# Turning heads and probabilities by VectorE and DRAM instead of by TensorE in a hybrid decoder layer

## The chip, the cores and the metric

The kernel runs on one core of a Trainium2 chip. The metric is device microseconds of one execution. Before the change the median of three runs is 1015.78 us (1015.49 to 1015.84). Engines are named as in the profile: PE is TensorE, DVE is VectorE, ACT is ScalarE, POOL is GpSimd, and SP is SyncE, which only issues transfers here.

## The reference: what is computed

One decoder layer over 256 tokens of width 2048, all in float32. A first RMS norm feeds one product with `w_in` (2048 to 4096 columns). Its columns are queries, keys and values of eight heads of 128, and 1024 columns for a pooling mixer.

```python
h = rms_norm(x, attn_norm_g)
q, k, v, p = jnp.split(h @ w_in, [1024, 2048, 3072], axis=-1)
q = rms_norm(heads(q), q_norm_g)          # per head, over its 128 columns
k = rms_norm(heads(k), k_norm_g)
a = moba_attention(q, k, heads(v), rel_bias)   # one block of 256: causal softmax with a T5 bias
m = multiscale_pool(p, pool_w, pool_scale)     # causal means over 2, 4, 8, 16 tokens, minus p, then a product
x = x + jnp.concatenate([a, m], axis=-1) @ w_out
x = x + conv_ffn(rms_norm(x, ffn_norm_g), w_up, conv_w, conv_b, w_down)
```

With 256 tokens there is one attention block, so every head is plain causal attention: scores `q k^T / sqrt(128)` plus a bias that depends on the distance, softmax, sum over values. The feed-forward part (width 5632, a causal convolution of three taps, a SiLU gate) is not touched by the change.

## The kernel before

**Weights.** All weights lie in DRAM in the order of their use, as 1 MB chunks of 128 x 2048. A chunk goes through four raw buffers (`raws`, transfers issued by SP). For accuracy each is split in two parts of a reduced float32 type: ACT writes the high part `wh` (L121), DVE writes the rest `wl` (L122). There are three buffers of each part. `split(c)` also issues the load of chunk c + 4 into the raw buffer that has come free (`release`).

**Steps.** The program is a list of steps, each with half a chunk of weight products (24 steps for chunks 0 to 11, and so on). At every even step u the split of chunk u/2 + 2 is issued, then what was `deferred` in the step before, then the products of the step, then the hooks that `after(u, f)` put behind it. So the order of each engine is written out by hand through these numbers. An engine executes its instructions in this order, and a waiting instruction holds all behind it on its engine.

**First part of the layer.** Steps 0 to 15 multiply x with 1024 columns at once, for all of the values v. Steps 16 to 47 are four blocks of eight steps (`tok_block`), each with 512 columns, that is four heads: keys, queries of heads 0 to 3, then keys, queries of heads 4 to 7. Steps 48 to 63 are four groups of pool columns, then come `w_out` and the feed-forward part.

**Attention.** At the end of a block `head_norm` takes the product from PSUM: ACT squares it, DVE sums, a short chain of ACT and DVE makes 1/sqrt, and DVE multiplies into an SBUF tile with tokens on the partitions. The scores need the head's columns on the partitions. `head_T` turns the four heads of a block on PE, eight transposes of 128 x 128 (L371), and ACT copies them out of PSUM with the gain of the norm as its scale (L372). For each head then follow, two steps apart from head to head: `scores` (two products on PE, L383; bias and maximum on DVE, L388; the exponentials on ACT are deferred), `normalise` (DVE, L400 and L402), `probs_T` (three transposes on PE, L409; a copy by ACT, L411) and `head_out` (two products with v, L419 and L420, then a split into the tile `cat` by ACT and DVE). The bias tile T for four heads is loaded by POOL from a small table in DRAM (L293); these eight transfers and the one that writes the table are all that POOL issues.

**Windows.** For each pool group DVE adds up windows of 2 to 16 tokens by doubling (`window_sums`), then `window_mean` multiplies with a table of 1/count (L458) and subtracts the token itself (L459).

## Time and profile before

| | |
|---|---|
| median of three runs | 1015.78 us (1015.49 to 1015.84) |
| profiled execution, its own time | 1015.66 us |
| span of that execution | 1013.9 us |
| granted TensorE clock, mean | 0.999 of full speed |
| PE busy, instructions | 1008.8 us, 5786 |
| DVE busy, instructions | 701.2 us, 760 |
| ACT busy, instructions | 512.5 us, 533 |
| POOL busy, instructions | 13.5 us, 31 |
| moved by transfers | 199.21 MB, mean 196 GB/s |

The span is the time from the first to the last instruction that the profiler saw; the execution's own time holds some start and end around it. Busy time of an engine is the time in which it had at least one instruction in work. The profile also follows the chain that ended last, backwards from the last instruction: at each step to what released it, or to the instruction before it on its engine.

### The profile page before, as it was taken

What the parts mean: (1) busy time and instruction counts of PE and PEld (TensorE: products, weight loads), DVE (VectorE), ACT (ScalarE), POOL (GpSimd) and SP (SyncE); (2) the same over time, 40 slices, a digit from 0 to 9 for tenths busy, and PEclk for the clock granted to TensorE, in tenths of its full rate; (3) what the DMA queues carried; (4) which work ended last, traced back from release to release, by engine and by line L of the source; (5) the groups of instructions that cost most, each with busy time, mean ns of one, the idle gap of its engine ahead of it and who ended that gap; (6) DMA issues with size and microseconds to landing.
All of it is one profiled execution on the core that took longest, in us unless ns stands there. A gap on an engine that the chain in (4) does not pass through costs nothing.

```text
span 1013.9 us, 13827 instructions
## 1 busy us (share of the span) xinstructions
PE 1008.8 (100%) x5786; PEld 887.0 (87%) x5786; DVE 701.2 (69%) x760; ACT 512.5 (51%) x533; POOL 13.5 (1%) x31
## 2 busy tenths in 40 slices
PE   9999999999999999999999999999999999999998
PEld 7888888898888888888888888888888888888888
DVE  6755668967768777777555677777755567777763
ACT  6644455556546555455434455555444445456431
POOL 0300000000000000000000000000000000000000
PEclk9999999999999999999999999999999999999999
DMA  8874454465554655555655555655555555555651
GB/s 338 305 253 166 166 187 167 166 249 208 172 211 175 220 178 206 197 180 193 207 187 202 190 185 189 207 186 197 197 194 202 184 190 194 195 193 180 216 185 42
DMA packets 31182, 199.21 MB, mean 196 GB/s; under 512 B 3640, under 2 KB 4920, under 8 KB 8208
## 3 DMA queue, kind: packets, MB, share of 16 engines
q1 hardware_dynamic: 30544, 196.89, 54.7%
q0 software_dynamic: 576, 1.44, 0.7%
q8 instruction: 45, 0.74, 0.3%
q14 instruction: 17, 0.14, 0.0%
HBM read 195.83 MB, written 2.49 MB: 196 GB/s over the span
## 4 chain that ended last, share of the span: by engine, by line
PE 98%; DMA 1%; SPq 0%; DVE 0%; ACT 0%; issue 0%
PE ps_feat L185 55%; PE ps_feat L187 28%; PE ps_tok L178 9%; PE ps_val L168 4%; PE ps_feat L194 1%; DMA raw<-in_wts 1%; PE ps_pool L194 1%; PE ps_s L383 1%; PE ps_T L371 0%; PE ps_av L419 0%; PE ps_eT L409 0%; SPq L111 0%; PE ps_av L420 0%; SPq L215 0%; PE ps_row L313 0%; DVE wl L122 0%
## 5 line engine op out<-in xcount | busy, mean ns | idle before, releaser
L122 DVE TENSOR_TENSOR wl<-raw,wh 128x2048 fp32r<-128x2048 f32 (+3 forms) x189 | 415.8, 2201 | 196.2 <-ACT wh L121 195.9
L185 PE MATMUL ps_feat<-x2h,wh 128*128 128x512 f32 x1408 | 479.1, 389 | 0.0
L121 ACT ACTIVATE wh<-raw 128x2048 fp32r<-128x2048 f32 (+3 forms) x189 | 348.0, 1842 | 103.3 <-PE ps_feat L185 59.9
L187 PE MATMUL ps_feat<-x2h,wl 128*128 128x256 f32 x1408 | 388.6, 276 | 0.0
L185 PEld LDWEIGHTS ps_feat<-x2h,wh 128*128 128x128 f32 x1408 | 264.3, 188 | 54.9
L187 PEld LDWEIGHTS ps_feat<-x2h,wl 128*128 128x128 f32 x1408 | 264.3, 188 | 0.0
L185 PE MATMUL ps_feat<-hid,wh 128*128 128x512 f32 x680 | 231.3, 389 | 0.0
L187 PE MATMUL ps_feat<-hid,wl 128*128 128x256 f32 x680 | 187.7, 276 | 0.0
L185 PEld LDWEIGHTS ps_feat<-hid,wh 128*128 128x128 f32 x680 | 127.6, 188 | 26.4
L187 PEld LDWEIGHTS ps_feat<-hid,wl 128*128 128x128 f32 x680 | 127.6, 188 | 0.0
L435 ACT ACTIVATE fs<-ps_feat 128x512 f32<-128x512 f32 x75 | 44.9, 598 | 157.3 <-PE ps_feat L187 157.3
L185 PE MATMUL ps_feat<-cat,wh 128*128 128x512 f32 x256 | 87.6, 390 | 0.0
L436 DVE TENSOR_TENSOR fs<-ps_feat,fs 128x512 f32<-128x512 f32 x75 | 51.7, 689 | 49.7 <-ACT fs L435 47.2
L178 PE MATMUL ps_tok<-wh,xh 128*128 128x512 f32 x256 | 82.0, 395 | 0.0
L187 PE MATMUL ps_feat<-cat,wl 128*128 128x256 f32 x256 | 70.7, 276 | 0.0
L677 ACT ACTIVATE hid<-y 128x512 fp32r<-128x512 f32 x22 | 13.9, 632 | 86.2 <-DVE y L676 86.2
L185 PEld LDWEIGHTS ps_feat<-cat,wh 128*128 128x128 f32 x256 | 48.1, 188 | 10.1
L178 PEld LDWEIGHTS ps_tok<-wh,xh 128*128 128x128 f32 x256 | 48.1, 188 | 9.9
L650 ACT ACTIVATE y<-u,pv 128x256 f32<-128x256 f32 x88 | 47.8, 591 | 5.6 <-DVE u L641 5.6
L178 PE MATMUL ps_tok<-wl,xh 128*128 128x512 f32 x128 | 49.9, 390 | 0.0
L187 PEld LDWEIGHTS ps_feat<-cat,wl 128*128 128x128 f32 x256 | 48.0, 188 | 0.0
L664 ACT ACTIVATE y<-y 128x512 f32<-128x512 f32 x22 | 13.9, 632 | 63.9 <-DVE y L653 63.9
(113 smaller groups left out, 681.3 us busy)
## 6 DMA issues: line engine op xcount, KB each, us to landing
raw<-in_wts SPq DMA_DIRECT2D x178, 1024.0 KB, 4.8
raw<-in_wts SPq DMA_DIRECT2D x4, 512.0 KB, 7.5
out<-x SPq DMA_DIRECT2D x7, 256.0 KB, 2.1
xboth<-in_xT SPq DMA_DIRECT2D x6, 256.0 KB, 10.0
T<-band POOLq DMA_DIRECT2D x8, 128.0 KB, 6.2
x<-in_xT SPq DMA_DIRECT2D x1, 1024.0 KB, 9.4
raw<-in_wts SPq DMA_DIRECT2D x3, 256.0 KB, 3.8
x<-in_xT SPq DMA_DIRECT2D x1, 768.0 KB, 7.4
```

The costliest lines, as they stand in the source:

```text
L121: nc.scalar.activation(wh, w, AF.Copy)
L122: nc.vector.tensor_tensor(wl, w, wh.bitcast(F32), op=OP.subtract)
L168: nc.tensor.matmul(ps[b][:, t, :], xh[:, k, a, ts], w[:, ws], start=False, stop=(k == KT - 1 and n == 2), skip_group_check=True)
L178: nc.tensor.matmul(ps[:, t, :], act[:, k0 + k, a, ts], w[:, ws], start=(first and k == 0 and n == 0), stop=(last and k == 1 and n == 2))
L185: nc.tensor.matmul(ps, wh[:, ws], act[:, k, :, :], start=(first and n == 0), stop=False, skip_group_check=True)
L187: nc.tensor.matmul(ps[:, S:], wl[:, ws], act[:, k, 0, :], start=False, stop=(last and n == len(ks) - 1), skip_group_check=True)
L194: nc.tensor.matmul(ps, w[:, ws], act[:, k, a, :], start=(first and n == 0 and i == 0), stop=(last and n == len(ks) - 1 and i == 2))
L435: nc.scalar.activation(dst, ps[:, :, S:], AF.Copy)
L436: nc.vector.tensor_tensor(dst, ps[:, :, :S], dst, op=OP.add)
L650: nc.scalar.activation(y[:, m, :], u[:, m, 2:], AF.Identity, scale=cw[2], bias=col(C_CB + f))
L664: nc.scalar.activation(y, y, AF.Silu)
L677: nc.scalar.activation(hid[:, ks, 0, :], y, AF.Copy)
```

## The change

Heads and probabilities are no longer turned on PE. DVE transposes blocks of 32 x 32 within their 32 partitions (`turn`), a transfer writes the result to DRAM (`store`), and four transfers, one for each group of 32 partitions, read it back so that the blocks stand where a full transpose would have put them (`land`). In the tile that arrives, the tokens of one head lie 8 elements (32 bytes) apart for queries and keys, and 3 elements (12 bytes) apart for probabilities. PE's score and value products read these tiles with such strides. Heads are stored through POOL and read back through SP; probabilities go both ways through POOL.

The order of the blocks changes with it. Steps 0 to 15 now make keys and queries of heads 0 to 3, steps 16 to 31 keys and queries of heads 4 to 7, steps 32 to 47 the values. `raw_heads` copies a block out of PSUM first; the norm runs from that copy some steps later. Both gains of the norms are folded in one scale that ACT applies to the keys in place after they have landed (`gains`). Scores of heads 0 to 3 stand at steps 31, 33, 35, 37 (before at 35 to 41), of heads 4 to 7 at 45 to 51 (before at 51 to 57). A head's sum over values comes ten steps after its scores (nine for heads 4 to 7; before six).

Apart from that, the table of the window mean covers only the first 16 tokens; the rest is a constant in one DVE instruction.

```diff
-        nc.vector.tensor_scalar(qs, col(C_QG), HD ** -0.5, None, op0=OP.mult)
+        nc.vector.scalar_tensor_tensor(qs, col(C_QG), HD ** -0.5, col(C_KG), op0=OP.mult, op1=OP.mult)
...
     def v_evac(ps, b):
-        for t in range(NT):
-            nc.scalar.activation(v[:, t, b * 512:(b + 1) * 512], ps[:, t, :], AF.Copy)
+        nc.scalar.activation(v[:, :, b * 512:(b + 1) * 512], ps, AF.Copy)
-    def head_norm(ps, name):
+    def raw_heads(ps, name):
+        n = early.tile([P, NT * 4, HD], F32, name=name + "n", tag="hn", bufs=3)
+        nc.scalar.activation(n, ps.rearrange("p t (h d) -> p (t h) d", d=HD), AF.Copy)
+        return n
+    def head_norm(n, name):
...
-        nc.scalar.activation(sq, psv, AF.Square)
+        nc.scalar.activation(sq, n, AF.Square)
...
-        nc.vector.tensor_tensor(n, psv, r[:, :, None].to_broadcast([P, NT * 4, HD]), op=OP.mult)
-        return n
-    def head_T(n, gc, name):
-        dst = early.tile([P, 4, S], F32, name=name, tag=name)
-        for i in range(2):
-            ps = aux("ps_T")
-            for j in range(2):
-                for t in range(NT):
-                    o = j * S + t * P
-                    nc.tensor.transpose(ps[:, o:o + P], n[:, t * 4 + 2 * i + j, :], ident)
-            nc.scalar.activation(dst[:, 2 * i:2 * i + 2, :], ps.rearrange("p (h t) -> p h t", t=S), AF.Copy, scale=gc)
+        nc.vector.tensor_tensor(n, n, r[:, :, None].to_broadcast([P, NT * 4, HD]), op=OP.mult)
+        return turn(n.rearrange("p n d -> p (n d)"), name, NT * 4)
+    def turn(src, name, n):
+        x = early.tile([P, 4, 32, n], F32, name=name + "x", tag="hn" if n == 8 else "ex", bufs=3 if n == 8 else 2)
+        nc.vector.transpose(x.rearrange("p j b n -> p n j b"), src.rearrange("p (n j b) -> p n j b", j=4, b=32))
+        return x, dram.tile([P, 4 * n * 32], F32, name=name + "d", tag=name + "d")
+    def store(xd, queue):
+        x, d = xd
+        queue.dma_start(d, x.rearrange("p j b n -> p (j b n)"))
+    def land(dst, xd, n, queue):
+        d = xd[1]
+        for j in range(4):
+            src = bass.AP(tensor=d.tensor, offset=d.offset + j * n * 32,
+                          ap=[[4 * n * 32, 32], [32 * 4 * n * 32, 4], [1, n * 32]])
+            queue.dma_start(dst[32 * j:32 * j + 32], src)
+    def head_T(d, name, queue):
+        dst = early.tile([P, P, NT * 4], F32, name=name, tag=name)
+        land(dst.rearrange("p (i b) n -> p i (b n)", b=32), d, NT * 4, queue)
         return dst
+    def gains(b):
+        k = st["kT", b].rearrange("p t n -> p (t n)")
+        nc.scalar.activation(k, k, AF.Copy, scale=qs)
...
-            nc.tensor.matmul(ps[:, s], qT[:, j, t * P:(t + 1) * P], kT[:, j, :(t + 1) * P],
+            nc.tensor.matmul(ps[:, s], qT[:, :, 4 * t + j], kT[:, :, j:4 * t + j + 1:4].rearrange("p b t -> p t b"),
...
+    def probs_turn(h):
+        hst[h] = turn(hst[h][0], f"e{h}", 3)
     def probs_T(h):
-        e = hst[h][0]
-        ps = small("ps_eT")
-        for b in range(3):
-            nc.tensor.transpose(ps[:, b * P:(b + 1) * P], e[:, b * P:(b + 1) * P], ident)
-        eT = early.tile([P, L], F32, name="eT", tag="eT", bufs=2)
-        nc.scalar.activation(eT, ps[:, :L], AF.Copy)
+        d = hst[h]
+        eT = early.tile([P, P, 3], F32, name="eT", tag="eT", bufs=3)
+        land(eT.rearrange("p (i b) c -> p i (b c)", b=32), d, 3, nc.gpsimd)
...
-        nc.tensor.matmul(ps[:, :S], v[:, 0, hs], eT[:, :S], start=True, stop=False, skip_group_check=True)
-        nc.tensor.matmul(ps[:, P:S], v[:, 1, hs], eT[:, S:L], start=False, stop=True, skip_group_check=True)
+        nc.tensor.matmul(ps[:, :S], v[:, 0, hs], eT[:, :, :2].rearrange("p t c -> p c t"),
+                         start=True, stop=False, skip_group_check=True)
+        nc.tensor.matmul(ps[:, P:S], v[:, 1, hs], eT[:, :, 2], start=False, stop=True, skip_group_check=True)
...
-        nc.vector.tensor_tensor(s, cur[:, :, PAD:], icnt[:, g:g + 1, :].to_broadcast([P, 2, S]), op=OP.mult)
-        nc.vector.tensor_tensor(s, s, pa[0][:, :, PAD:], op=OP.subtract)
+        w = WINDOWS[g]
+        nc.vector.tensor_tensor(cur[:, :, PAD:PAD + w], cur[:, :, PAD:PAD + w],
+                                icnt[:, g:g + 1, :w].to_broadcast([P, 2, w]), op=OP.mult)
+        nc.vector.scalar_tensor_tensor(s, cur[:, :, PAD:], 1.0 / w, pa[0][:, :, PAD:], op0=OP.mult, op1=OP.subtract)
...
     for b in range(2):
-        for nm, gc in (("k", col(C_KG)), ("q", qs)):
-            after(st[nm, b, "end"] + (10 if b and nm == "k" else 3), lambda nm=nm, b=b, gc=gc: st.__setitem__(
-                (nm + "T", b), head_T(st[nm, b], gc, nm + "T")))
-        at = st["q", b, "end"] + 4
+        at = (31, 45)[b]
+        for nm, u0, u1 in (("k", (19, 26)[b], (24, 40)[b]), ("q", (22, 33)[b], (27, 41)[b])):
+            after(u0, lambda nm=nm, b=b: (st.__setitem__((nm, b), head_norm(st[nm, b], f"{nm}{b}")),
+                                          store(st[nm, b], nc.gpsimd)))
+            after(u1, lambda nm=nm, b=b: st.__setitem__(
+                (nm + "T", b), head_T(st[nm, b], nm + "T", nc.sync)))
+        after(at - 1, lambda b=b: gains(b))
         for j in range(4):
             h, u = 4 * b + j, at + 2 * j
             after(u, lambda h=h, b=b: scores(h, st["qT", b], st["kT", b], st["T", b]))
-            after(u + 2, lambda h=h: normalise(h))
+            after(u + 1, lambda h=h: (normalise(h), probs_turn(h), store(hst[h], nc.gpsimd)))
             after(u + 4, lambda h=h: probs_T(h))
-            after(u + 6, lambda h=h: head_out(h))
+            after(u + 10 - b, lambda h=h: head_out(h))
```

What the numbers do to the order is shown at three places. The first is PE where a block of the first part ends and attention work is let in between the weight products (`ps_tok`): before, around head 3's scores, with `ps_eT` the turned probabilities:

```order
L178 MATMUL ps_tok<-wh,xh 128x512
L419 MATMUL ps_av<-eT,v 128x256
L420 MATMUL ps_av<-eT,v 128x128
L409 MATMUL ps_eT<-ident,e 128x128 x3
L383 MATMUL ps_s<-kT,qT 128x128
L383 MATMUL ps_s<-kT,qT 128x256
L178 MATMUL ps_tok<-wh,xh 128x512
```

The same engine in the changed kernel, at step 45, where the value products of head 2 and the scores of head 4 meet:

```order
L178 MATMUL ps_tok<-wh,xh 128x512
L438 MATMUL ps_av<-eT,v 128x256
L440 MATMUL ps_av<-eT,v 128x128
L402 MATMUL ps_s<-kT,qT 128x128
L402 MATMUL ps_s<-kT,qT 128x256
L178 MATMUL ps_tok<-wh,xh 128x512
```

The transposes are gone from between the products, and nothing stands in their place.

The second place is DVE after step 33 in the changed kernel, from the scores of head 1 (`L407`) to the next weight split (`wl`); `m`, `rs_s` and `hr` are the norm's small tiles, `q1n` the queries of heads 4 to 7:

```order
L407 ISA mx 128x1
L407 ISA e,mx<-ps_s,T 128x256
L407 ISA mx 128x1
L409 TENSOR_SCALAR mx<-mx 128x2
L357 TENSOR_REDUCE m<-sq 128x8
L359 TENSOR_SCALAR m<-m,e_155 128x4 x2
L303 TENSOR_TENSOR rs_s<-rs_r 128x8
L304 SCALAR_TENSOR_TENSOR rs_s<-rs_s,m 128x8
L305 SCALAR_TENSOR_TENSOR hr<-rs_s,rs_r 128x8
L363 TENSOR_TENSOR q1n<-q1n,hr 128x1024
L369 STREAM_TRANSPOSE q1x<-q1n 128x8x128
L122 TENSOR_TENSOR wl<-raw,wh 128x2048
```

Between two splits now stand, beside the normalisation and block transpose of the head before, a score's maximum, a whole norm and a second block transpose; before, DVE had no transposes, and the norm of a block stood right after the block's last product.

The third place is SP, where loads of turned heads are let in between the loads of weights:

```order
+L111 DMA raw<-in_wts 128x2048 x5
+L382 DMA kT<-k0d 32x4x256 x4
+L111 DMA raw<-in_wts 128x2048
+L382 DMA qT<-q0d 32x4x256 x4
+L111 DMA raw<-in_wts 128x2048 x7
+L382 DMA kT<-k1d 32x4x256 x4
+L382 DMA qT<-q1d 32x4x256 x4
+L111 DMA raw<-in_wts 128x2048 x14
```

Before, one unbroken row of 27 weight loads stood here.

## The prediction

> **Bound now.** I read three views in this order: the page's busy times, its chain of waits, and the groups of the two engines that prepare the weights.

> ```profile
> span 1013.9 us, 13827 instructions
> PE 1008.8 (100%) x5786; PEld 887.0 (87%) x5786; DVE 701.2 (69%) x760; ACT 512.5 (51%) x533; POOL 13.5 (1%) x31
> ...
> PE 98%; DMA 1%; SPq 0%; DVE 0%; ACT 0%; issue 0%
> ...
> L122 DVE TENSOR_TENSOR wl<-raw,wh 128x2048 fp32r<-128x2048 f32 (+3 forms) x189 | 415.8, 2201 | 196.2 <-ACT wh L121 195.9
> ...
> L121 ACT ACTIVATE wh<-raw 128x2048 fp32r<-128x2048 f32 (+3 forms) x189 | 348.0, 1842 | 103.3 <-PE ps_feat L185 59.9
> ```

> PE owns 98% of the chain. VectorE's split of the weights (L122) waits for ScalarE's (L121), and that one waits for PE to give a buffer back. So the supply runs ahead of PE, and a microsecond taken off PE is a microsecond off the end, as long as nothing new makes PE wait. The chain in order of time (start, length, work) prices what PE does around the edit:

> ```profile
> 50.52 5.44 PE ps_tok L178 x24
> ...
> 55.96 0.43 PE ps_row L313 x2
> ...
> 80.91 0.87 PE ps_T L371 x8
> ...
> 107.21 0.66 PE ps_s L383 x4
> ...
> 119.50 0.33 PE ps_eT L409 x3
> ...
> 125.95 0.43 PE ps_av L419 x2
> 126.38 0.22 PE ps_av L420 x2
> 126.60 0.33 PE ps_eT L409 x3
> ...
> 155.77 0.87 PE ps_T L371 x8
> ```

> One step is 12 of those ps_tok products, 5.44/2 = 2.72 us. Between them PE stops for the transposes of the heads (0.87 us for eight), the scores (0.66), the transposes of the probabilities (0.33 for three) and the sums over values (0.43 + 0.22 = 0.65).

> **Removed.** From PE all transposes. The groups by shape count them:

> ```profile
> L409 PE MATMUL ps_eT<-ident,e 128*128 128x128 f32 x24 | 3.9, 272 | 0.0
> ...
> L371 PE MATMUL ps_T<-ident,kn 128*128 128x128 f32 x16 | 2.1, 272 | 0.0
> L371 PE MATMUL ps_T<-ident,qn 128*128 128x128 f32 x16 | 2.1, 272 | 0.0
> ```

> That is 32/8 = 4 groups of 0.87 us and 24/3 = 8 groups of 0.33 us: 3.5 + 2.6 = 6.1 us. The weight products are the same in number and shape; only which columns come first changes.

> **PE reads.** PE gets no new instruction, but the scores now read queries and keys 32 bytes apart, and the sums over values read probabilities 12 bytes apart. No row of before has PE reading with a stride. Lower bound: nothing. Upper bound: both kinds of product take twice as long, 8 x (0.66 + 0.65) = 10.5 us. I take nothing, for this reason: a score pass streams 128 + 128 + 256 + 256 = 768 columns in 0.66 us, 0.86 ns a column, while ps_tok streams 24 x 512 columns in 5.44 us, 0.44 ns each. These products take their columns at half the pace that the same ports reach elsewhere, so a read that is up to twice as slow would still keep up. [...] Reads that pay for their stride are the second rival.

> **VectorE.** It gets 4 transposes of 1024 elements per partition and 8 of 384. The nearest rows:

> ```profile
> L360 DVE TENSOR_TENSOR qn<-ps_tok,hr 128x1024 f32<-128x1024 f32 x2 | 2.4, 1224 | 0.2
> L402 DVE SCALAR_TENSOR_TENSOR e<-e,mx,rrow 128x256 f32<-128x256 f32 x4 | 1.9, 478 | 0.0
> ...
> L458 DVE TENSOR_TENSOR pst<-pa,icnt x4: 691/691/693, 167.3 to 204.0; 128x512 f32<-128x512 f32 x4
> ```

> I take 1.22 us for 1024 elements, and 0.58 for 384, between 0.48 (256) and 0.69 (512). That adds 4 x 1.22 + 8 x 0.58 = 9.5 us. The smaller window mean takes about 4 x 0.5 = 2 us off (four products of 512 become products of 4 to 32 elements, for which the row of 128x8 below has 0.17). Bounds: a block transpose at no more than these rows, or at four times them, since nothing in before transposes on VectorE. [...]

> The tightest place for VectorE is step 33, where the norm of the second queries and their transpose stand between two splits. The rows, in order of time:

> ```profile
> 73.85 1.22 DVE L353 TENSOR_REDUCE m<-sq 128x8 f32<-128x1024 f32 x1 [2.26 <-ACT sq L351]
> ...
> 75.98 0.17 DVE L303 TENSOR_TENSOR rs_s<-rs_r 128x8 f32<-128x8 f32 x1 [0.52 <-ACT rs_r L302]
> ...
> 76.65 1.22 DVE L360 TENSOR_TENSOR kn<-ps_tok,hr 128x1024 f32<-128x1024 f32 x1
> ...
> 107.91 0.29 DVE L388 CUSTOM_DVE_ANT_0 e<-ps_s,T 128x128 f32<-128x128 f32 x1 [2.77 <-PE ps_s L383]
> ...
> 108.58 0.17 DVE L390 TENSOR_SCALAR mx<-mx 128x2 f32<-128x2 f32 x1
> ...
> 111.41 0.16 DVE L400 RECIPROCAL mx<-mx 128x2 f32<-128x2 f32 x1
> 111.60 0.75 DVE L402 SCALAR_TENSOR_TENSOR e<-e,mx,rrow 128x128 f32<-128x128 f32 x2
> ...
> L351 ACT ACTIVATE sq<-ps_tok x4: 1024/1026/1027, 72.8 to 146.0; 128x1024 f32<-128x1024 f32 x4
> ```

> Count from the end of step 31 on PE. ScalarE copies the second queries out (about 1.03, as L351) and splits (1.84 by the first fence's L121), VectorE splits (2.20, L122): 5.1 us. Normalise 0.9 (111.60 + 0.75 - 111.41), transpose 0.58: 6.6. Scores of head 1, 108.58 + 0.17 - 107.91 = 0.84: 7.4. Norm, 76.65 + 1.22 - 73.85 = 4.0, and its transpose 1.22: 12.6. The next split 2.20: 14.8. PE wants it when step 38 begins, 6 x 2.72 + 3 x 0.66 = 18.3. Margin 3.5 us: no wait, even with transposes of twice the length (16.6). Later, where heads 4 to 7 and the window sums meet, before was the tighter:

> ```profile
> 160.00:180.00 20.00, 20.00 (x122) 17.79 (x121) 19.45 (x38) 11.10 (x22) 0.00 (x0) 1.00 0.46 159
> ```

> From 160 to 180 us VectorE (its busy time comes third, after PE and the weight loads) was at 19.45 of 20 us and PE still at 20.00. The change starts heads 4 to 7 six steps earlier (45, not 51), which thins this stretch. So VectorE's additions are hidden under PE's weight products. Cost taken: nothing.

> **ScalarE** loses 8 copies of transposed heads and 8 of probabilities:

> ```profile
> L372 ACT ACTIVATE kT<-ps_T,pv x4: 678/684/688, 81.4 to 153.2; 128x512 f32<-128x512 f32 x4
> L411 ACT ACTIVATE eT<-ps_eT x8: 472/491/492, 122.6 to 192.8; 128x384 f32<-128x384 f32 x8
> ```

> 8 x 0.68 + 8 x 0.49 = 9.4 us go; four copies of raw heads and two scalings of keys of about 1.03 come, 6.2 us. It is lighter, and at 51% off the path.

> **Queues.** A transposed head must leave by POOL and come back by SP; probabilities do both by POOL.

> ```profile
> T<-band POOLq DMA_DIRECT2D x8, 128.0 KB, 6.2
> raw<-in_wts SPq DMA_DIRECT2D x178, 1024.0 KB, 4.8
> xboth<-in_xT SPq DMA_DIRECT2D x6, 256.0 KB, 10.0
> band<-rsb POOLq DMA_DIRECT2D x1, 384.0 KB, 10.1
> ...
> DMA to landing us min/median/max: 4.7/6.2/9.0
> ...
> DMA to landing us min/median/max: 4.7/5.0/5.6
> ...
> 49.49 2.18 POOL L293 DMA_DIRECT2D T<-band  x4 [9.58 <-DMA band<-rsb]
> ...
> 49.76 0.42 SPq L276 DMA_DIRECT2D icnt<-in_icnt  x1
> ```

> The T tiles (landing 4.7 to 9.0 us, the last four of them 4.7 to 5.6) have the very shape of a head's load: 32 partitions, 4 x 1 KB each. POOL issues one in 2.18/4 = 0.55 us; a head now asks for five (2.8 us) in 5.4 us or more, so POOL keeps up. Probabilities leave after step 32 and are wanted after 41 (head 0), or after 46 and 54 (head 4): 8 steps or more, 21.8 us, for two landings of at most 10.1. The heads' stores have 5 steps or more, 13.6 us, before their load. The table for the window mean shrinks from 512 KB to 32 and leaves SP sooner. T of heads 0 to 3 now stands behind two stores on POOL, but has until step 31.

> The queries are the tight ones. First half: chunk 12 frees its buffer at 50.52 + 10 x 2.72 + 0.43 = 78.2 us; ScalarE and VectorE split chunk 15 by 82.2; SP issues one weight load and four parts of queries, five times 0.42, by 84.3; with 4.7 to 9.0 to land they are there at 89.0 to 93.3. The scores stand at 50.52 + 16 x 2.72 + 0.43 = 94.5. Margin 1.2 to 5.5. Second half, from the end of step 39: copy of values 1.03, splits 4.0, nine issues 3.8, so 8.9; landed at 13.6 to 17.9; wanted after step 45 at 6 x 2.72 + 3 x 0.65 = 18.3. Margin 0.4 to 4.7. Behind a late load stands more than the scores: the scaling of keys waits on ScalarE for the keys, and with it the next split. Cost taken: nothing; bounds nothing and, at a landing of 12 us, 1.8 + 2.6 = 4.4 us. Weight loads have room: one is issued when its buffer's chunk is split, four chunks or 8 x 2.72 = 21.8 us before its own split, and lands in 4.8.

> **Sum.** -6.1 + 0 + 0 + 0. The profiled execution took 1015.66 us, span 1013.9 and 1.8 around it; the span would be 1007.8 and the time 1009.6. The median of the runs, 1015.78, lies 0.1 higher: 1009.7 us.

> **Rivals.**
> First: the queries or keys land late and PE waits at steps 31 and 45. For it: margins of 1.2 and 0.4 us against the slowest T, and that SP's queue puts them right behind a 1 MB weight load, where the 256 KB parts of x took 10.0 us. Against it: the later T tiles' 4.7 to 5.6. At 12 us it gives 1009.7 + 4.4 = 1014.1.
> Second, the other side: PE's strided reads are slower than 0.86 ns a column. It decides from a factor of 1 + 6.1/10.5 = 1.6 on scores and sums; at two it gives 1009.7 + 10.5 = 1020.2, slower. For it: no strided read of PE in before; against it: the half pace.
> Third: a block transpose takes four times the row (4.9 and 2.3 us). The split at step 38 then comes at 14.8 + 3.7 + 1.7 = 20.2, 1.9 us late, and the crowd at step 51 may cost about as much again: 1013.5. For it: writes 32 bytes apart; against it: nothing shown.
> Fourth: the change does not do what it says, since PE spends the freed time in short waits for splits: about 1015.8. Against it: PE at 20.00 of 20 us beside a full VectorE.

> **Numbers.** Forecast 0.55 (its own range 1008.5 to 1011), late landing 0.20 (1011 to 1016), strided reads 0.14, slow transposes 0.07, no effect 0.04. Runs of before lie within 0.35 us; no change means within 0.2%, 2.0 us. Faster: the forecast, 0.12 of late landing and 0.03 of the rest, 0.70. Same: 0.08 of late landing, 0.04 of strided reads, 0.05 of the rest, 0.17. Slower: the strong forms of the second and third rival, 0.13. The range goes from 1008.5 to 1016.5, which leaves out the stronger half of strided reads, the worst transposes and a little below.

> **Signs.** Right: no ps_T and ps_eT in the chain, ps_s at 0.66 us and ps_av at 0.43 + 0.22, PE without idle time before ps_s. Wrong: a wait of PE for the loads of qT or kT (first rival), ps_s or ps_av longer in the chain (second), a STREAM_TRANSPOSE above 2.4 us with PE waiting for wl (third).

## The result and the profile after

The changed kernel is slower: 1026.33 us median of four runs (1025.14 to 1027.61) against 1015.81 of before in the same session; ratio 1.0105, 95% interval 1.0093 to 1.0118. The forecast was 1009.7. The profiled execution took 1027.24 us, 11.6 more than that of before.

The head of the page and its shares of the chain of waits, after:

```profile
span 1025.4 us, 13829 instructions
...
PE 1015.9 (99%) x5730; PEld 887.8 (87%) x5730; DVE 712.2 (69%) x772; ACT 510.3 (50%) x521; POOL 34.1 (3%) x75
...
PE 92%; DMA 4%; DVE 2%; issue 1%; ACT 0%; SPq 0%; DVEq 0%
```

PE has 56 products fewer (5730, not 5786) and is yet busy for 7.1 us more. Its share of the chain fell from 98% to 92%: other work now ends last at some places. The chain in order of time (start, length, work) shows both:

```profile
78.26 2.30 DVE wl L122
80.57 8.84 DMA raw<-in_wts
89.43 0.30 SPq L382
89.77 7.95 DMA qT<-q0d
97.85 1.74 PE ps_s L402 x4
99.59 7.56 PE ps_tok L178 x24
107.16 1.39 PE ps_s L402 x4
108.55 5.48 PE ps_tok L178 x24
...
132.97 10.82 DMA raw<-in_wts
143.80 4.30 DMA qT<-q1d
...
148.34 1.74 PE ps_s L402 x4
...
155.55 0.68 PE ps_av L438 x2
156.22 0.35 PE ps_av L440 x2
156.57 1.43 PE ps_s L402 x4
...
163.68 1.50 PE ps_s L402 x4
```

The scores of one head take 1.39 us and more where before they took 0.66, the sums over values 0.68 + 0.35 = 1.03 where they took 0.65. Twice a load of queries stands ahead of the scores, and ahead of that load a load of weights (`raw`), which VectorE's split (`wl`) had released: SP issued the last queries only when those weights had landed (80.57 + 8.84 = 89.41). The block of weight products behind the first of these two waits takes 7.56 us instead of 5.48. No ps_T and no ps_eT is left. The groups by shape (count, then busy us and mean ns of one, then idle time before it and what ended it) say which instructions grew:

```profile
L402 PE MATMUL ps_s<-kT,qT 128*128 128x256 f32 x16 | 8.8, 643 | 0.0
L438 PE MATMUL ps_av<-eT,v 128*128 128x256 f32 x16 | 6.7, 504 | 0.0
L402 PE MATMUL ps_s<-kT,qT 128*128 128x128 f32 x16 | 5.7, 443 | 4.5 <-DMA qT<-q0d 3.4 <-DMA qT<-q1d 1.2
L440 PE MATMUL ps_av<-eT,v 128*128 128x128 f32 x16 | 4.1, 340 | 0.0
...
L369 DVE STREAM_TRANSPOSE k0x<-k0n 128x1024 f32<-128x1024 f32 x1 | 2.1, 2145 | 0.0
```

In the same view of before, the products of 256 columns had 380 ns (scores) and 377 (sums over values), those of 128 columns 274. The two waits, 3.4 and 1.2 us, are in the third row.

The sum from these rows, for PE: transposes gone -6.1; eight heads' scores, 1.39 x 3 + 1.43 + 1.50 x 2 + 1.74 x 2 = 12.1 instead of 8 x 0.66 = 5.3, so +6.8; sums over values 8 x (1.03 - 0.65) = +3.0; waits 3.4 + 1.2 = +4.6; the block behind the first wait 7.56 - 5.48 = +2.1. That makes +10.4. The medians lie 10.5 apart; the spans of the two profiled executions, from which the rows come, lie 11.5 apart, so that 1.1 us stays outside these rows.

### The profile page after: what moved, and what is told of

Read it like the earlier page. It is cut to its first block, busy times and chain, and to the rows that moved or that the text cites. A ratio compares the mean times of both kernels' runs of the same rounds, so it can differ in the third digit from the quotient of the medians.

```text
span 1025.4 us, 13829 instructions
## 1 busy us (share of the span) xinstructions
PE 1015.9 (99%) x5730; PEld 887.8 (87%) x5730; DVE 712.2 (69%) x772; ACT 510.3 (50%) x521; POOL 34.1 (3%) x75
## 4 chain that ended last, share of the span: by engine, by line
PE 92%; DMA 4%; DVE 2%; issue 1%; ACT 0%; SPq 0%; DVEq 0%
PE ps_feat L185 55%; PE ps_feat L187 27%; PE ps_val L168 4%; PE ps_tok L178 3%; DMA raw<-in_wts 3%; PE ps_s L402 1%; DVE wl L122 1%; PE ps_feat L194 1%; DMA qT<-q0d 1%; PE ps_pool L194 1%; DMA qT<-q1d 0%; PE ps_av L438 0%; ACT wh L121 0%; DVE m L357 0%; SPq L111 0%
## 5 line engine op out<-in xcount | busy, mean ns | idle before, releaser
L122 DVE TENSOR_TENSOR wl<-raw,wh 128x2048 fp32r<-128x2048 f32 (+3 forms) x189 | 415.6, 2201 | 185.5 <-ACT wh L121 185.4
L185 PE MATMUL ps_feat<-x2h,wh 128*128 128x512 f32 x1408 | 479.1, 389 | 0.0
L121 ACT ACTIVATE wh<-raw 128x2048 fp32r<-128x2048 f32 (+3 forms) x189 | 348.0, 1842 | 99.9 <-PE ps_feat L185 64.6
L185 PEld LDWEIGHTS ps_feat<-x2h,wh 128*128 128x128 f32 x1408 | 264.3, 188 | 54.9
L185 PE MATMUL ps_feat<-hid,wh 128*128 128x512 f32 x680 | 231.3, 389 | 0.0
L185 PEld LDWEIGHTS ps_feat<-hid,wh 128*128 128x128 f32 x680 | 127.6, 188 | 26.5
L185 PE MATMUL ps_feat<-cat,wh 128*128 128x512 f32 x256 | 87.5, 390 | 0.0
L178 PE MATMUL ps_tok<-wh,xh 128*128 128x512 f32 x256 | 84.6, 406 | 0.0
L178 PEld LDWEIGHTS ps_tok<-wh,xh 128*128 128x128 f32 x256 | 49.3, 192 | 10.8
L185 PEld LDWEIGHTS ps_feat<-cat,wh 128*128 128x128 f32 x256 | 48.0, 188 | 10.2
L178 PE MATMUL ps_tok<-wl,xh 128*128 128x512 f32 x128 | 50.7, 396 | 0.0
L185 PE MATMUL ps_feat<-xh,wh 128*128 128x512 f32 x128 | 47.4, 412 | 0.0
## 6 DMA issues: line engine op xcount, KB each, us to landing
raw<-in_wts SPq DMA_DIRECT2D x178, 1024.0 KB, 4.8
out<-x SPq DMA_DIRECT2D x7, 256.0 KB, 4.5
xboth<-in_xT SPq DMA_DIRECT2D x6, 256.0 KB, 9.2
T<-band POOLq DMA_DIRECT2D x8, 128.0 KB, 7.7
x<-in_xT SPq DMA_DIRECT2D x1, 1024.0 KB, 8.5
raw<-in_wts SPq DMA_DIRECT2D x3, 256.0 KB, 3.6
```

Source lines behind the costliest of these rows:

```text
L121: nc.scalar.activation(wh, w, AF.Copy)
L122: nc.vector.tensor_tensor(wl, w, wh.bitcast(F32), op=OP.subtract)
L178: nc.tensor.matmul(ps[:, t, :], act[:, k0 + k, a, ts], w[:, ws], start=(first and k == 0 and n == 0), stop=(last and k == 1 and n == 2))
L185: nc.tensor.matmul(ps, wh[:, ws], act[:, k, :, :], start=(first and n == 0), stop=False, skip_group_check=True)
```

## The experiments

Two causes were in view: strided reads of PE (about 9.8 us) and queries that land late (about 6.7 us with what follows). Each was taken away alone, then each was taken apart.

**Consecutive reads.** The two products read the same tiles with the same sizes, but consecutive columns. This leaves out picking the right columns.

```diff
-  qT[:, :, 4 * t + j], kT[:, :, j:4 * t + j + 1:4].rearrange("p b t -> p t b")
+  qf[:, (4 * t + j) * P:(4 * t + j + 1) * P], kf[:, j * P:(j + t + 1) * P]     # qf, kf: qT, kT flat
-  eT[:, :, :2].rearrange("p t c -> p c t") ... eT[:, :, 2]
+  ef[:, :S] ... ef[:, S:L]                                                      # ef: eT flat
```

> The changed kernel, but PE's scores and sums over values read consecutive columns of the same tiles instead of columns 32 or 12 bytes apart; it leaves out picking the right columns, so its numbers are not the layer's. Everything else, loads and order included, is the change's. Theory stride: the scores fall from 1.39 us (1.74 after a wait) to 0.66 and the sums from 1.03 to 0.65, 6.8 + 3.0 = 9.8 us off 1026.3, so 1016.5. Rival, the products are long because of what stands around them (late loads, a lower clock): they stay near 1.4 and 1.0 us and the time near 1026.

Measured: 1018.92 us (1018.39 to 1021.88), ratio 1.0032 (1.0021 to 1.0043). The chain of this kernel:

```profile
97.67 0.89 PE ps_s L403 x4
...
104.05 0.66 PE ps_s L403 x4
...
143.82 1.27 PE ps_s L403 x4
145.09 6.71 PE ps_tok L178 x24
151.80 0.43 PE ps_av L440 x2
```

With consecutive columns a score is back at 0.66 us and a sum over values at 0.43 + 0.22, as before the change, except right behind a wait. So the stride is the cause of the longer products. The waits did not go (2.5 us for the first queries, 3.0 for the second), and here it is the second that has a slow block behind it, 6.71 us. Waits and slow block together make 5.5 + 1.2 = 6.7 us, as in the change (4.6 + 2.1), so they are not why the time is 2.4 us above what was expected. Of that, 0.8 us are the two scores behind a wait, which stay longer (0.89 and 1.27), and 0.9 us come about because the expectation set rows of the change's profiled execution (1027.24) against its median (1026.33). The last 0.7 us were not located.

**Scores two steps later.** The scores, and with them all that counts from them, are put at steps 33 and 47.

```diff
-        at = (31, 45)[b]
+        at = (33, 47)[b]
```

> The changed kernel with the scores of each half two steps later (33 and 47 for 31 and 45), and all that hangs on them. Theory wait: the loads of queries land before PE asks, the 3.4 + 1.2 us of idle time before the scores go and with them the 2.1 us in which the clock was lower after the first pause: 6.7 us off, 1019.6. Rival, the loads come late again because they stand in queues in the program's order, and the idle time moves along: 1024 to 1027. By the theory stride alone the scores keep their 1.39 us in both cases.

Measured: 1019.39 us (1018.74 to 1019.65), ratio 1.0031 (1.0020 to 1.0042). Its chain:

```profile
84.94 14.97 PE ps_tok L178 x66
99.91 1.39 PE ps_s L402 x4
...
161.82 1.50 PE ps_s L402 x4
```

PE waits for no transfer of queries or keys, the scores stay at 1.39 to 1.50 us and the sums at 1.02. The waits (4.6) and the slow block behind (2.1) make 6.7 of the 6.9 us between the medians of this kernel and the change. The two causes are separate: without the strided reads PE still loses 6.7 us to the waits and what follows, and without the waits the scores of all heads still take 11.4 us (before 5.3) and the sums 3.0 us more. So the strides alone cost 6.1 + 3.0 = 9.1 us.

**Which operand pays.** Heads 0 to 3 read only the stationary operand (queries) 32 bytes apart, heads 4 to 7 only the moving one (keys). The sums over values read consecutive columns for heads 0 to 3, columns 8 bytes apart for heads 4 to 7. This too leaves out picking the right columns.

```diff
+  q1, k1 = qT[:, :, 4 * t + j], kf[:, j * P:(j + t + 1) * P]
+  if h >= 4:
+      q1 = qf[:, (4 * t + j) * P:(4 * t + j + 1) * P]
+      k1 = kT[:, :, j:4 * t + j + 1:4].rearrange("p b t -> p t b")
 ...
```

> The changed kernel, but heads 0 to 3 read the keys (the moving operand) from consecutive columns and keep the stride for the queries (the stationary one), heads 4 to 7 the other way round; sums over values read consecutive columns for heads 0 to 3 and columns 8 bytes apart for heads 4 to 7. It leaves out picking the right columns. If the moving operand pays, scores take 0.66 to 0.7 us for heads 0 to 3 and 1.2 to 1.4 for heads 4 to 7; if the stationary one pays, the reverse; if both, about 1.0 each. [...]

Measured: 1022.51 us, one run. The chain:

```profile
105.69 0.94 PE ps_s L407 x4
...
161.69 1.38 PE ps_s L407 x4
...
184.47 0.45 PE ps_av L449 x2
184.92 0.23 PE ps_av L451 x2
```

Heads 5 to 7, with the moving operand alone strided, take 1.38 us; the same heads took 1.43 and 1.50 in the change. Heads 1 to 3, with the stationary one alone, take 0.94, which neither expectation had: 0.94 - 0.66 = 0.28 us a head. Where both are strided most of this is covered: nothing of it shows in heads 1 to 3 of the change (1.39), 0.05 to 0.12 us in heads 5 to 7. Columns 8 bytes apart are nearly free: 0.45 + 0.23 = 0.68 instead of 0.65. PE waited here too, 2.8 and 2.4 us, with slow blocks of 7.09 and 6.93 us behind.

**The price as a function of the stride.** With the later scores as base, the moving operand is read 16 bytes apart (heads 0 to 3) or 8 bytes apart (heads 4 to 7), the stationary one consecutively. Some of the block transposes write consecutive elements. This again leaves out picking the right columns.

```diff
+  m = 4 if h < 4 else 2
+  k1 = kf[:, :m * (t + 1) * P].rearrange("p (c m) -> p c m", m=m)[:, :, 0]
 ...
+  if name in ("k1", "q1", "e4", "e5", "e6", "e7"):
+      xo = x.rearrange("p j b n -> p (j b n)").rearrange("p (n j b) -> p n j b", j=4, b=32)
```

> Scores two steps later (as in e2_later), with a consecutive stationary operand; the moving operand is read 16 bytes apart for heads 0 to 3 and 8 bytes apart for heads 4 to 7. The block transposes of k1, q1 and of the probabilities of heads 4 to 7 write consecutive elements; those of k0, q0 and heads 0 to 3 write 32 and 12 bytes apart as in the change. This leaves out picking the right columns. Line theory (a read pays about 1.8 ns whenever it opens a new 16 bytes, and nothing as long as two elements come from one): the two products of a head take 1.38 us at 16 bytes, the same as at 32, and 0.66 to 0.70 us at 8 bytes; time 1019.4 - 4 x 0.7 = 1016.6 us. Rival (the cost grows with the stride): about 1.0 us at 16 bytes and 0.75 at 8; time 1019.4 - 4 x 0.39 - 4 x 0.63 = 1015.3 us. Transposes: if the strided write is what makes 1024 elements take 2.15 us and 384 take 0.70, the consecutive ones take about 1.2 and 0.58 us (before's duration for a VectorE pass of that width); if the transpose itself is slow, they stay at 2.15 and 0.70.

Measured: 1016.49 us, one run. Its chain, and then its groups by shape:

```profile
107.44 1.36 PE ps_s L408 x4
...
154.59 0.68 PE ps_s L408 x4
```

```profile
L372 DVE STREAM_TRANSPOSE q0x<-q0n 128x1024 f32<-128x1024 f32 x1 | 2.1, 2150 | 0.0
...
L372 DVE STREAM_TRANSPOSE q1x<-q1n 128x1024 f32<-128x1024 f32 x1 | 1.2, 1246 | 0.0
...
L372 DVE STREAM_TRANSPOSE e0x<-e 128x384 f32<-128x384 f32 x1 | 0.7, 695 | 0.0
...
L372 DVE STREAM_TRANSPOSE e6x<-e 128x384 f32<-128x384 f32 x1 | 0.6, 579 | 0.0
```

At 16 bytes a head costs 1.36 us, as at 32 bytes; at 8 bytes 0.68. From 16 to 32 bytes the cost does not grow with the stride; it fits a count of how often a new piece of 16 bytes is opened. A head's scores stream 768 columns: at 16 bytes 1.36/768 = 1.77 ns for each, one opening per column; at 32 bytes, in the change, 1.39/768 = 1.81. The sums over values in the change, 12 bytes apart, open 0.75 per column: 0.75 x 1.77 = 1.33 ns, and measured are 0.68/512 = 1.33. At 8 bytes it is 0.5 x 1.77 = 0.89 and measured are 0.68/768 = 0.89, hardly more than the 0.86 of consecutive float32 columns. One price fits four strides: 0.68 us a head with two columns to a piece, 1.36 with one. The piece of 16 bytes was an assumption of the expectation; the fit to these four strides is what the runs show of it.

The block transposes pay for strided writes too: 2.15 us at 32 bytes and 1.25 when written consecutively, 0.70 at 12 bytes and 0.58.

**Heads loaded by POOL.** The heads' loads leave SP, where they stand between weight loads, and go out on POOL one or two steps earlier.

```diff
-  (("k", (19, 26)[b], (24, 40)[b]), ("q", (22, 33)[b], (27, 41)[b]))
+  (("k", (19, 26)[b], (22, 39)[b]), ("q", (22, 33)[b], (25, 40)[b]))
-  head_T(st[nm, b], nm + "T", nc.sync)
+  head_T(st[nm, b], nm + "T", nc.gpsimd)
```

> The changed kernel with the heads' loads issued by POOL instead of SP, and hung on steps 22, 25, 39, 40 instead of 24, 27, 40, 41; SP issues weights alone. Theory queue: what made the queries late is SP, where they stand behind a weight load and wait for its landing before they are issued (5.4 us between first and last issue of the first queries). Then the idle time before the scores goes: 6.7 us off, 1019.6. Rival, the transfer engines are simply full there (busy share 1.02 to 1.09 from 84 to 96 us): landing stays near 9 to 11 us, at least 2 us of idle time stay, 1022 or more.

Measured: 1027.78 us (1026.31 to 1030.28), ratio 1.0117 (1.0098 to 1.0135), no better than the change. Its waits (engine, line, what it waited for; us in all, times, longest):

```profile
PE ps_s L402 <- DMA eT<-e3d: 7.2, 1, 7.2
...
PE ps_s L402 <- DMA qT<-q0d: 0.6, 1, 0.6
```

The first wait fell from 3.4 to 0.6 us, though the loads of the first queries still took 7.5 to 9.3 us, with T in the same stretch. Their first issue was as late as in the change (84.3 us), but the last left at 85.9 instead of 89.8, with no weight load between. The keys' loads, too, had moved, from 81.0 to 71.6 us, so this run does not take SP apart from the crowd. In the second half the heads' loads stood on POOL among those of T and of probabilities, and POOL held issues back until earlier transfers had landed (3.6, 0.7 and 2.5 us). PE waited 7.2 us, which the profile puts down to a load of probabilities. So POOL was no way out.

**T out of the way.** What shares the engines with the first queries? Transfers in the change by stretches of 4 us; the columns are busy times of PE, PEld, DVE, ACT, POOL, then the granted clock, the DMA share (1 is all 16 engines) and GB/s:

```profile
88.00:92.00 4.00, 4.00 (x19) 3.34 (x18) 3.84 (x3) 2.32 (x2) 0.56 (x1) 1.00 1.09 289
...
96.00:100.00 4.00, 2.15 (x6) 1.82 (x7) 0.37 (x3) 1.36 (x1) 0.00 (x0) 0.64 1.03 376
100.00:104.00 4.00, 4.00 (x11) 3.11 (x10) 3.90 (x8) 1.94 (x5) 0.00 (x0) 0.51 0.47 156
```

The engines are full there, at shares of 1.03 to 1.09 from 88 to 100 us. The loads of T for heads 0 to 3, issued at 49.5 us before the change, now go out behind step 24, at 79.3 us, just ahead of it. One edit moves them to step 17.

```diff
-    after(24, lambda: st.__setitem__(("T", 0), bias_tile(0)))
+    after(17, lambda: st.__setitem__(("T", 0), bias_tile(0)))
```

> The change with one edit: the loads of the position bias T of heads 0 to 3 are issued after step 17 instead of after step 24, and so leave the stretch from 80 to 100 us in which queries and keys come back. If the crowd on the DMA engines makes the queries late: the 3.4 us wait before the first scores falls under 1 us, the block behind it is back at 5.5 us, and the time is 1026.3 - 3.4 - 2.1 = 1020.8 us (up to 1023 if a part of the wait is left). If it is the order of issue on SP's queue alone, where the queries' four loads stand between weight loads: the wait stays at 3 to 3.5 us and the time at 1026. The wait of 1.2 us in the second half stays in both.

Measured: 1021.94 us (1021.49 to 1022.87), ratio 1.0061 (1.0047 to 1.0075). Its chain:

```profile
55.91 38.12 PE ps_tok L178 x168
94.17 1.74 PE ps_s L402 x4
...
138.88 3.71 DMA qT<-q1d
142.83 1.74 PE ps_s L402 x4
144.57 6.62 PE ps_tok L178 x24
```

PE now runs from 55.91 into the first scores with no wait. So without T in that stretch the first queries come in time. T had made them late in two ways. The queries that SP issued first now landed in 9.4 us instead of 11.6 to 11.9; and the weight load on whose landing SP waits landed in 6.6 us instead of 8.84, so that the last queries were issued at 87.2 us instead of 89.8. The engines stay full from 84 to 96 us all the same (shares of 1.03 to 1.08), so the share alone does not tell how late a load will be. In the second half 1.4 us of waiting stay, and the slow block (6.62 us) has moved there; this is why 4.4 us were won and not 5.5. In the change the issue itself is late in both halves; SP's row for the second (start, length from the first to the last issue, work) and its waits:

```profile
135.56 8.55 SPq L382 DMA_DIRECT2D qT<-q1d  x4
```

```profile
SPq L382 <- DMA raw<-in_wts: 11.2, 2, 6.9
```

SP held the queries' loads back until weight loads had landed, 6.9 us here and 4.3 us in the first half, and the four issues were spread over 8.55 us, where the prediction had 0.42 each. In the second half of the change the first three loads of queries, issued by 136.4 us, had landed by 147.5, and the held one at 148.1. If it had landed with the others, about 0.6 of the 1.2 us of waiting would be left, an estimate from these times that no run tested.

**Another layout, without either cost.** The turned data lie in DRAM and SBUF as runs of 32 tokens, instead of tokens interleaved by head. The transfers stay the same in size and number, keys and probabilities are read in runs of 128 bytes, and the block transposes write consecutively. ACT's pass for the gains goes to the queries, which it writes in order as the stationary operand, and not to the keys; no pass is added. The scores stand two steps later.

```diff
-  x = early.tile([P, 4, 32, n], ...);  nc.vector.transpose(x.rearrange("p j b n -> p n j b"), ...)
+  x = early.tile([P, 4, n, 32], ...);  nc.vector.transpose(x.rearrange("p j n b -> p n j b"), ...)
-  dst = early.tile([P, P, NT * 4], ...);  eT = early.tile([P, P, 3], ...)
+  dst = early.tile([P, 4, NT * 4, 32], ...);  eT = early.tile([P, 4, 3, 32], ...)
-  nc.scalar.activation(k, k, AF.Copy, scale=qs)
+  nc.scalar.activation(qd.rearrange("p n (i b) -> p n i b", b=32), qT.rearrange("p i n b -> p n i b"), AF.Copy, scale=qs)
-  qT[:, :, 4 * t + j], kT[:, :, j:4 * t + j + 1:4].rearrange("p b t -> p t b")
+  qd[:, 4 * t + j, :], kT[:, :, j:4 * t + j + 1:4, :].rearrange("p i t b -> p t i b")
-  eT[:, :, :2].rearrange("p t c -> p c t") ... eT[:, :, 2]
+  eT[:, :, :2, :].rearrange("p i c b -> p c i b") ... eT[:, :, 2, :]
-        at = (31, 45)[b]
+        at = (33, 47)[b]
```

> The change with another layout of the turned data (32 consecutive tokens in a run instead of tokens 32 or 12 bytes apart): the block transposes write consecutive elements, keys and probabilities are read by TensorE in runs of 128 bytes, and ScalarE's pass for the gains goes to the queries and writes them consecutively, so that no pass is added. Scores two steps later, as in e2_later. If strided reads and late landings are the whole of what went wrong: the scores back at 0.66 us a head, the sums of probabilities and values at 0.65, no wait of TensorE before the scores, and the 6.1 us of the removed transposes are left: 1015.8 - 6.1 = 1009.7 us, between 1009 and 1011. Rival, that reads pay for every run that they begin (four of 128 bytes for each 128 columns): 0.1 us more for each product, 16 products, 1011.3 us. Rival, that some cost of the round trip besides these two is not seen yet: 1013 us or more.

Measured: 1010.17 us (1010.11 to 1010.38, five runs) against 1015.64, ratio 0.9944 (0.9931 to 0.9958). It beats both kernels. Its groups by shape:

```profile
L404 PE MATMUL ps_s<-kT,qd 128*128 128x256 f32 x16 | 4.8, 380 | 0.0
L440 PE MATMUL ps_av<-eT,v 128*128 128x256 f32 x16 | 4.7, 378 | 0.0
...
L404 PE MATMUL ps_s<-kT,qd 128*128 128x128 f32 x16 | 3.1, 274 | 0.0
L442 PE MATMUL ps_av<-eT,v 128*128 128x128 f32 x16 | 3.1, 274 | 0.0
...
L392 ACT ACTIVATE qd<-qT,qs 128x1024 f32<-128x1024 f32 x2 | 2.3, 1145 | 1.5 <-DMA qT<-q1d 1.5
```

Each product has its duration of before the change, and PE waits for no load of queries, keys or probabilities. Both rivals are ruled out, since they asked for 1011.3 and for 1013 us or more. Beginning a run of 128 bytes costs nothing that can be seen in these rows (380 and 274 ns for the scores, as before the change). ACT's reordering pass takes 1145 ns, about as long as the plain scaling of the keys that it replaces (1153 ns in the change). Of the 6.1 us, 5.5 arrive; the weight products of the pool columns (`ps_feat<-xh`), among which heads 4 to 7 now end, are busy for 0.9 us more (46.1 + 35.6 instead of 45.4 + 35.4), which is about the size of what is missing. Why they are was not taken apart. Between the median with the scores two steps later alone (1019.39) and this one lie 9.2 us, the price of the strides again. The layout was not run without the later scores.

## Why the prediction was wrong, point by point

**Removed, -6.1 us: right.** No ps_T or ps_eT remains, and the last kernel gains 5.5 us of it once the other two costs are gone.

**PE reads, taken as nothing: the step that failed first.** It cost 6.8 + 3.0 = 9.8 us, 9.1 where nothing waits, close to its upper bound of 10.5; the run without waits, 1019.39, is close to the second rival's 1020.2. The argument was that float32 products take a column in 0.86 ns where those of `ps_tok` take one in 0.44, so a read twice as slow would keep up. The first half of this fits the runs: 0.86 is about twice 0.44, and at 8 bytes apart a read costs next to nothing (0.68 us a head instead of 0.66). The gap is in "up to twice as slow". That was assumed of any stride; a column 32 bytes apart costs 1.81 ns, four times the 0.44 and twice the 0.86. The half pace was a reason for 8 bytes, not for 32, and no row of a strided read backed the argument.

**VectorE, hidden: right for PE's own waits, wrong for the loads.** The transposes took 2.15 and 0.70 us instead of 1.22 and 0.58, because of the strided writes. PE never waited for a `wl` in the attention part, so the third rival did not come about. But VectorE had little slack before the first queries: the chain that ends in the first wait runs through its norms, transposes and splits up to the split at 78.26, and that split releases the weight load at 80.57 whose landing SP waits for. In the last kernel, where the two transposes of the first keys and queries take 1.25 us each, this weight load leaves at 78.8 us instead of 80.5 (the same order with strided writes, scores two steps later), and the last queries at 86.8 instead of 89.0. So the longer transposes were not hidden; they were part of why the queries came late.

**ScalarE, lighter: right in sign.** 510.3 us busy instead of 512.5.

**Queues, taken as nothing: the step that failed second.** The first rival came about beside the second, not instead of it; its price at the bound, 4.4 us, is near the 4.6 us of waiting, but that is luck, since it was 1.8 + 2.6 in the two halves and 3.4 + 1.2 were measured. The time at which the first scores would stand was right: 94.5 forecast, 97.85 - 3.35 = 94.50 without the wait. Wrong was the arrival: 89.0 to 93.3 forecast, 97.7 measured (89.77 + 7.95). Three terms were mis-sized. The issues were taken at 0.42 us each, the last by 84.3 us; SP waited 4.3 us between them for a weight load to land and issued the last one at 89.8. That one landed in 7.95 us, inside the forecast. The landing was taken from T tiles of before at 4.7 to 9.0 us; the first two loads of queries, issued at 84.2 and 84.6, took 11.6 and 11.9 and landed at 95.8 and 96.5, where the scores stood at 94.5, so they were late by themselves. The medians of four (KB each, us from issue to landing):

```profile
qT<-q0d SPq DMA_DIRECT2D x4, 128.0 KB, 9.8
...
qT<-q1d SPq DMA_DIRECT2D x4, 128.0 KB, 10.8
```

And the T tiles' own move into the same stretch was noted only for its deadline, not for what it does to its neighbours; the run with T at step 17 shows that the first wait goes without it.

**Not priced: the granted clock.** The slow block behind a wait, 2.1 us in the change, had no term: a late landing was priced as its length alone. The clock granted to PE was 0.64 and 0.51 of full speed from 96 to 104 us.

**The odds and the range.** Strided reads got 0.14, late landing 0.20, each as a case by itself. They have different causes, so they could fall together, and the upper bounds of the two terms, 10.5 and 4.4, belonged together into the range: 1009.7 + 14.9 = 1024.6. The 2.1 us of the slow block come on top.

## What to carry to other kernels

Price a strided read of PE by how many 16-byte pieces it opens (1.77 ns for each fits these runs), not by an average pace, measure what a strided write adds (here 2.15 us instead of 1.25 for 1024 elements), and look for a layout whose innermost run is long; here the same round trip with 32 tokens in a run, and with the scores two steps later, turned 10.5 us lost into 5.5 us won. A landing time holds only for the traffic beside which it was measured (4.7 to 9.0 us for the T tiles before, 11.6 and 11.9 for the first loads of queries, of the same size, in the change): when a plan moves transfers, draw up what else flies in the same stretch, and what must land before the queue issues the load at all (SP held queries back for 4.3 and 6.9 us). And give a data round trip that ends in front of PE two steps of margin, since a wait of PE can cost more than its length (in the change 3.4 us, and 2.1 more in the block behind).
